# Forgetting attention of six heads issued in the written order on every engine and queue

## The chip, the core and the metric

The kernel runs on one NeuronCore of a Trainium2 chip. The metric is device microseconds (us) of one execution, lower is better. The engines of the core are named as in the profile: PE (matrix products and transposes), DVE (vector engine), ACT (scalar engine), POOL, and SP, whose queue issues all the DMAs of this kernel. Each engine takes its own instructions in the order in which they stand in its program; an instruction whose semaphore has not come yet holds up all that stand behind it on the same engine or queue.

## The reference

One layer of a hybrid decoder on 2048 tokens of width 1024: a normalised, modulated input is projected, three groups of heads mix it (a matrix memory, forgetting attention, spatial gating), an output projection follows, then a convolutional feed-forward block. The part that the change touches is the attention, eight heads of width 64:

```python
F = jnp.cumsum(jax.nn.log_sigmoid(f_pre.astype(jnp.float32)), axis=-1)
for blk in range(s_len // Q_BLOCK):                 # 16 blocks of 128 queries
    lo, hi = blk * Q_BLOCK, (blk + 1) * Q_BLOCK
    logits = (jnp.einsum('bhtd,bhsd->bhts', q[:, :, lo:hi], k[:, :, :hi]) * scale
              + F[:, :, lo:hi, None] - F[:, :, None, :hi])
    logits = jnp.where(mask, logits, -jnp.inf)      # causal
    p = jax.nn.softmax(logits, axis=-1)
    outs.append(jnp.einsum('bhts,bhsd->bhtd', p, v[:, :, :hi]))
```

## The kernel before

The program is written with a framework that sets the semaphores, gives the tiles their buffers, and by default also orders the instructions of each engine: its scheduler takes the written program, and where an instruction is not ready by its own reckoning, it puts a later one that is ready ahead of it. Inside a `tc.manual_schedule()` block every engine and queue keeps the written order instead. The kernel already uses this block for most of the input projections; the attention stands outside it.

The attention runs over heads h = 0 to 7 and, inside a head, over four blocks tb of 512 queries: `phase((h, tb), ...)`. Heads 1 to 6 take tb = 0, 1, 2, 3 in this order; head 0 has only tb = 2 and 3 left here, since its first two blocks are made beside the last input projection; head 7 takes 2, 3, 0, 1.

**`scores` (L190 on).** A block has four rows of 128 queries. A row sees `(tb*4+i+1)*128` keys, taken in parts of at most 1024 columns. One unit is one part: PE makes the logits in a PSUM tile `sp` (L206, two buffers; for 512 columns two products, of the high and the low half of q, then the causal mask by L210), and DVE adds the forget bias and takes the row's extreme in one custom instruction (L212). So a block has 4, 4, 8 and 8 units for tb = 0, 1, 2, 3. When the last part of a row is written, its exponentials follow on ACT (`exps`, L223, one for each part) and the division by the row sum on POOL (L225, L226, L228). These stand in the code behind the `yield` of the unit, so that they are written only when the next unit is asked for.

**`finish` (L234 on).** The product with v, for one block of 128 keys at a time, `(tb+1)*4` units. A unit transposes up to four tiles of the probabilities on PE (L259, into `tp`, three buffers), ACT copies the result as the high half `phi` (L262), DVE subtracts it for the low half `plo` (L263), and PE multiplies both halves with `vv` (L245, L246). The product is held back by three units (the list `behind`): unit j writes the transposes of j and then the product of j-3. There is one PSUM buffer `op` for a block's product; after its last product ACT copies it out as `yo` (L250), and two DMAs store it (L252).

**`phase` (L269 on)** interleaves the scores of one block with the finish of the block before it:

```python
nxt = order[order.index(now) + 1]
kv[nxt] = load_q(*nxt, "qB")                  # four DMAs of q for the next block
n_fin = sum(4 * (t[1] + 1) for t in then)     # units of the block that is finished
for n in range(n_sc):                         # n_sc = 4, 4, 8 or 8 units of scores
    next(sc)
    while done < (n + 1 - lead) * (n_fin - 5) // (n_sc - lead):
        next(fin)
        done += 1
for _ in sc: pass                             # the exponentials of the last row
for _ in fin: pass                            # the rest of the finish
```

So in the written order phase (h, 0) has 2, 3, 3, 3 units of finish behind its four units of scores, phase (h, 1) none (n_fin - 5 is negative), phase (h, 2) 0, 0, 1, 0, 0, 1, 0, 1, phase (h, 3) 0 and then one behind each, and each phase ends with the four or five units of finish that are left.

After the first phase of a head, `load_k(h + 1)` and `load_v(h + 1, range(4))` write the loads of the next head: two DMAs of `kk` (L157), one of `nf` (L158), four of `vv` (L163, 256 KB each). The tag `kvB` has six buffers, three for a head, so head h+1 takes the buffers of head h-1 from h = 2 on. The `q` tiles (tag `qB`, L173, 128 KB for a DMA) have four buffers, two for a block.

Behind the attention stand the output projection (whose weights are loaded by `load_w(0)` in the sixth head), the up projection with its convolution, and the down projection; all of them keep the scheduler's order.

Of the kernel before, what the change touches and what calls it, by code (L numbers as in the profile page):

```python
# [21 lines left out]
NH = 8  # L22
# [11 lines left out]
def trunk(  # L34
# [116 lines left out]
    def load_k(h):  # L151
        tag, e = "kvA" if h == 0 else "kvB", slice(h % 2 * 64, h % 2 * 64 + 64)
        kk = pool.tile([P, S], F32R, name="kk", tag=tag)
        nf = pool.tile([P, S], F32, name="nf", tag=tag)
        vv = pool.tile([P, S // P, P], F32R, name="vv", tag=tag)
        for i in range(2):
            dma(kk[64 * i : 64 * i + 64].bitcast(F32), k_d[h // 2, i, e])  # L157
        dma(nf, nf_d[h : h + 1, :].broadcast_to([P, S]))  # L158
        kv[h] = kk, nf, vv

    def load_v(h, cs):
        for c in cs:
            dma(  # L163
                kv[h][2][:, 4 * c : 4 * c + 4].bitcast(F32),
                v_d[c * TB : (c + 1) * TB, h, :].rearrange("(n p) d -> p n d", p=P),
            )

    def load_q(h, tb, tag):
        q2 = []
        for n in range(2):  # L170
            t = pool.tile([P, TB], F32R, name="q", tag=tag)
            for i in range(2):
                dma(  # L173
                    t[64 * i : 64 * i + 64].bitcast(F32),
                    q_d[h // 2, n, h % 2 * 64 : h % 2 * 64 + 64, tb * TB : (tb + 1) * TB],
                )
            q2.append(t)
        return q2
# [55 lines left out]
    def finish(h, tb, rows):  # L234

        ns = (tb + 1) * 4
        vv = kv[h][2]

        got = []

        def product(j, c0, hi, lo):
            if j == 0:
                got.append(pp.tile([P, 512], F32, name="op", tag="op"))
            op = got[0]
            T.matmul(op[:, c0:], vv[:, j, :], hi[:, c0:], start=(j == 0), stop=False)  # L245
            T.matmul(op[:, c0:], vv[:, j, :], lo[:, c0:], start=False, stop=(j == ns - 1))  # L246
            if j == ns - 1:
                yo = pool.tile([P, 512], F32, name="yo", tag="yo")

                A.copy(yo, op)  # L250
                for n, d in enumerate((yt_d, y2_d)):
                    dma(d[h * 64 : h * 64 + 64, tb * TB : (tb + 1) * TB], yo[64 * n : 64 * n + 64])  # L252

        for j in range(ns):
            i0 = max(0, j - tb * 4)
            c0 = i0 * P
            tp = pp.tile([P, 512], F32, name="tp", tag="tp")
            for i in range(i0, 4):
                T.transpose(tp[:, i * P : (i + 1) * P], rows[i][j // 8][:, (j % 8) * P : (j % 8 + 1) * P], ident)  # L259
            hi = pool.tile([P, 512], F32R, name="phi", tag="phl")  # L260
            lo = pool.tile([P, 512], F32R, name="plo", tag="phl")
            A.copy(hi[:, c0:], tp[:, c0:])  # L262
            V.tensor_tensor(lo[:, c0:], tp[:, c0:], hi[:, c0:].bitcast(F32), op=ALU.subtract)  # L263
            behind.append(lambda j=j, c0=c0, hi=hi, lo=lo: product(j, c0, hi, lo))
            if len(behind) > 3:
                behind.pop(0)()
            yield

    def phase(now, then, lead=0):  # L269

        rows = []
        sc, n_sc = iter(()), 0
        if now:
            sc, n_sc = scores(*now, kv.pop(now) if now in kv else load_q(*now, "qB"), rows), (4, 4, 8, 8)[now[1]]
            if now in order and now != order[-1]:
                nxt = order[order.index(now) + 1]
                kv[nxt] = load_q(*nxt, "qB")
        n_fin = sum(4 * (t[1] + 1) for t in then)
        fin = (u for t in then for u in finish(*t))
        done = 0  # L280
        for n in range(n_sc):
# [4 lines that stand above are left out]
        for _ in sc:  # L286
            pass
        for _ in fin:
            pass
        return now and [(*now, rows)]  # L290

    def wout_open_right():
        pool.open("wo_r", "right", ("yhl0", 2048, 16), ("ld", 2048, 3), ("wo0", 2048, 16))

    def load_split(src, tag, eng, more=None):
        t = pool.tile([P, TB], F32, name="ld", tag="ld")
        dma(t, src)
        if more is not None:
            t2 = pool.tile([P, TB], F32, name="ld", tag="ld")
            dma(t2, more)  # L300
            eng.tensor_tensor(t, t, t2, op=ALU.add)
        hi = pool.tile([P, TB], F32R, name=tag + "h", tag=tag)
        lo = pool.tile([P, TB], F32R, name=tag + "l", tag=tag)
        split(hi, lo, t, eng)
        return hi, lo
# [3 lines left out]
    def load_w(nb):  # L309
        for k in range(KT):  # L310
            src = w_out[k * P : (k + 1) * P, nb * 512 : nb * 512 + 512]
            wo.append(load_split(src, "wo%d" % nb, (G, V)[k % 2]))
# [757 lines left out]
    written = ExitStack()  # L1070
# [57 lines left out]
    for h in range(NH):  # L1128
        for n, tb in enumerate(TBS if h == NH - 1 else (2, 3) if h == 0 else range(4)):
            if (h, n) == (NH - 2, 1):  # L1130
                pool.close("att_r")
                wout_open_right()
            if (h, n) == (NH - 2, 3):
                load_w(0)
            last = phase((h, tb), last, 3 if (h, n) == (0, 0) else 0)
            if n == 0 and h < NH - 1:
                load_k(h + 1)
                load_v(h + 1, range(4))
# [607 lines left out]
```

## Time and profile before

| what | value |
|---|---|
| median of the runs | 2610.47 us (three runs, 2605.68 to 2610.91) |
| profiled execution | 2607.8 us, span of its instructions 2606.1 us |
| mean granted clock of PE | 0.997 |
| the scores' products on PE, first to last | 672.8 to 1111.3 us |
| period of a head, heads 1 to 4 | 51.66 to 51.68 us |

The attention takes the stretch from about 700 to 1125 us of the span, a sixth of the time; the phases that the change touches, (0, 3) to (5, 3), have their scores on PE between 724.7 and 996.7 us. The profile's line numbers (L206 and so on) are those of the kernel before; in the changed kernel all lines behind L1134 stand four lower.

### The profile page before, as it was taken

What the parts mean: (1) busy time and instruction counts of PE and PEld (TensorE: products, weight loads), DVE (VectorE), ACT (ScalarE), POOL (GpSimd) and SP (SyncE); (2) the same over time, 40 slices, a digit from 0 to 9 for tenths busy, and PEclk for the clock granted to TensorE, in tenths of its full rate; (3) what the DMA queues carried; (4) which work ended last, traced back from release to release, by engine and by line L of the source; (5) the groups of instructions that cost most, each with busy time, mean ns of one, the idle gap of its engine ahead of it and who ended that gap; (6) DMA issues with size and microseconds to landing.
All of it is one profiled execution on the core that took longest, in us unless ns stands there. A gap on an engine that the chain in (4) does not pass through costs nothing.

```text
span 2606.1 us, 36311 instructions
## 1 busy us (share of the span) xinstructions
PE 2530.5 (97%) x12521; PEld 2097.9 (81%) x12537; DVE 2010.0 (77%) x3438; ACT 1272.8 (49%) x2424; POOL 402.5 (15%) x532
## 2 busy tenths in 40 slices
PE   5999999999999999999989999999999999999999
PEld 5888888888787877777868888888888888888787
DVE  7657666476388889866589888888888887997797
ACT  4333343432388878844455544454444444444443
POOL 2012310132266556520000000000000000000000
PEclk9999999999999999999999999999999999999999
DMA  7345763454664445266632222255222217658523
GB/s 247 107 120 160 209 209 88 129 152 138 180 164 123 129 126 166 58 195 224 248 89 92 79 89 82 81 201 187 90 81 81 90 65 279 210 176 290 184 93 117
DMA packets 302592, 379.58 MB, mean 146 GB/s; under 512 B 31934, under 2 KB 194588, under 8 KB 300360
## 3 DMA queue, kind: packets, MB, share of 16 engines
q1 hardware_dynamic: 302408, 377.26, 46.1%
q8 instruction: 99, 1.62, 0.3%
q14 instruction: 85, 0.70, 0.1%
HBM read 276.44 MB, written 100.74 MB: 145 GB/s over the span
## 4 chain that ended last, share of the span: by engine, by line
PE 81%; DVE 9%; DMA 4%; ACT 3%; issue 2%; POOL 1%; SPq 0%; DVEq 0%; ACTq 0%; POOLq 0%
PE ub L56 11%; PE ub L54 11%; PE ub L55 11%; PE acc L54 6%; PE acc L56 6%; PE acc L55 6%; PE db L55 4%; PE db L56 4%; PE db L54 4%; PE sp L206 3%; PE tp L259 3%; PE op L245 2%; PE op L246 2%; PE wps L55 2%; PE wps L54 2%
## 5 line engine op out<-in xcount | busy, mean ns | idle before, releaser
L54 PE MATMUL acc<-wh,hh 128*128 128x512 f32 (+2 forms) x768 | 285.5, 373 | 1.9 <-DVE vhl L762 1.2
L54 PE MATMUL ub<-T,wsph 128*128 128x512 f32 x704 | 274.2, 390 | 5.8 <-ACT wsph L1358 5.8
L56 PE MATMUL ub<-T,wspl 128*128 128x512 f32 x704 | 273.7, 389 | 1.6 <-DVE wspl L1359 1.6
L56 PE MATMUL acc<-wh,hl 128*128 128x512 f32 (+2 forms) x768 | 274.2, 360 | 0.3 <-DVE hl L566 0.3
L55 PE MATMUL acc<-wl,hh 128*128 128x512 f32 (+2 forms) x768 | 273.9, 358 | 0.2
L55 PE MATMUL ub<-T,wsph 128*128 128x512 f32 x704 | 273.9, 389 | 0.0
L55 PE MATMUL db<-wspl,wsph 128*128 128x512 f32 x616 | 240.6, 391 | 3.6 <-DVE wspl L1490 3.5
L56 PE MATMUL db<-wsph,wspl 128*128 128x512 f32 x616 | 239.6, 389 | 0.0
L54 PE MATMUL db<-wsph 128*128 128x512 f32 x616 | 238.3, 389 | 0.3 <-ACT wsph L1489 0.3
L1358 ACT CAST wsph<-S 128x512 fp32r<-128x512 f32 x176 | 109.7, 623 | 228.4 <-PE ub L55 162.8
L263 DVE TENSOR_TENSOR plo<-tp,phi 128x512 fp32r<-128x512 f32 (+1 forms) x320 | 187.0, 607 | 31.6 <-ACT phi L262 29.4
L54 PE MATMUL ub<-B,wsph 128*128 128x512 f32 x528 | 207.1, 392 | 2.8 <-ACT wsph L1358 2.8
L56 PE MATMUL ub<-B,wspl 128*128 128x512 f32 x528 | 207.2, 392 | 0.6 <-DVE wspl L1359 0.6
L55 PE MATMUL ub<-B,wsph 128*128 128x512 f32 x528 | 207.0, 392 | 0.0
L223 ACT ACTIVATE L<-L,nm 128x1024 f32<-128x1024 f32 (+2 forms) x192 | 172.6, 903 | 36.0 <-DVE nm L212 34.7
L262 ACT CAST phi<-tp 128x512 fp32r<-128x512 f32 (+1 forms) x320 | 160.0, 521 | 40.2 <-PE tp L259 38.9
L259 PE MATMUL tp<-ident,L 128*128 128x128 f32 x1088 | 177.0, 274 | 2.5 <-POOL L L228 0.6
L206 PE MATMUL sp<-kk,q 128*128 128x512 f32 (+3 forms) x640 | 169.2, 375 | 3.3 <-DVE nm L212 2.2
L1489 ACT CAST wsph<-act 128x512 fp32r<-128x512 f32 x132 | 82.3, 623 | 179.0 <-PE db L55 162.2
L228 POOL TENSOR_SCALAR L<-L,rs 128x1024 f32<-128x1024 f32 (+2 forms) x192 | 167.2, 881 | 11.0
L56 PEld LDWEIGHTS acc<-wh,hl 128*128 128x128 f32 x768 | 145.0, 190 | 22.3 <-DVE hl L566 0.8
L54 PEld LDWEIGHTS acc<-wh,hh 128*128 128x128 f32 x768 | 146.2, 191 | 20.7 <-DVE vhl L762 1.4
(333 smaller groups left out, 5942.9 us busy)
## 6 DMA issues: line engine op xcount, KB each, us to landing
w<-in_w_up_dram SPq DMA_DIRECT2D x88, 512.0 KB
wd<-in_w_down_dram SPq DMA_DIRECT2D x176, 256.0 KB
wa<-in_w_ada_dram SPq DMA_DIRECT2D x96, 256.0 KB
act_d<-yc SPq DMA_DIRECT2D x44, 512.0 KB
act<-act_d SPq DMA_DIRECT2D x44, 512.0 KB
wr<-in_w_in_dram SPq DMA_DIRECT2D x64, 256.0 KB
q<-q_d SPq DMA_DIRECT2D x128, 128.0 KB
hc_d<-hl SPq DMA_DIRECT2D x28, 512.0 KB
```

Of the source, the lines that this page charges most:

```text
L54: T.matmul(ps, lh, rh, start=start, stop=False, skip_group_check=resume)
L55: T.matmul(ps, lh, rl, start=False, stop=False, skip_group_check=resume)
L56: T.matmul(ps, ll, rh, start=False, stop=stop, skip_group_check=resume)
L206: T.matmul(sp[:, b : b + bw], q2[n][:, qs], kk[:, s0 + b : s0 + b + bw], start=n == 0, stop=n == 1 and not last)
L223: A.activation(L[c], L[c], AF.Exp, bias=nm[:, n - 1 : n], scale=-1.0, accum_out=rs[:, c : c + 1])
L228: G.tensor_scalar(t, t, rs[:, 0:1], 1.0, op0=ALU.mult, op1=ALU.mult)
L245: T.matmul(op[:, c0:], vv[:, j, :], hi[:, c0:], start=(j == 0), stop=False)
L259: T.transpose(tp[:, i * P : (i + 1) * P], rows[i][j // 8][:, (j % 8) * P : (j % 8 + 1) * P], ident)
L262: A.copy(hi[:, c0:], tp[:, c0:])
L263: V.tensor_tensor(lo[:, c0:], tp[:, c0:], hi[:, c0:].bitcast(F32), op=ALU.subtract)
L1358: A.copy(hi, src)
L1489: A.copy(hi, v)
```

## The change

Four lines in the loop over the phases. The block of written order is entered ahead of phase (0, 3), the second of head 0, and left ahead of phase (6, 0). In between, PE, DVE, ACT, POOL and SP's DMA queue keep the order in which the code writes them. No instruction is added, removed or changed in size.

```diff
             if (h, n) == (NH - 2, 3):
                 load_w(0)
+            if (h, n) == (0, 1):
+                written.enter_context(tc.manual_schedule())
+            if (h, n) == (NH - 2, 0):
+                written.close()
             last = phase((h, tb), last, 3 if (h, n) == (0, 0) else 0)
             if n == 0 and h < NH - 1:
                 load_k(h + 1)
                 load_v(h + 1, range(4))
```

## The prediction

> **What bounds the kernel now.** I read the page first, then the stretches of single heads, the groups by form in the attention, the waits, and last the order in time of PE, DVE, ACT and SP.
>
> ```profile
> span 2606.1 us, 36311 instructions
> PE 2530.5 (97%) x12521; PEld 2097.9 (81%) x12537; DVE 2010.0 (77%) x3438; ACT 1272.8 (49%) x2424; POOL 402.5 (15%) x532
> PE 81%; DVE 9%; DMA 4%; ACT 3%; issue 2%; POOL 1%; SPq 0%; DVEq 0%; ACTq 0%; POOLq 0%
> ...
> core 0: us, PE busy (x) PEld busy (x) DVE busy (x) ACT busy (x) POOL busy (x), PEclk, DMA share, GB/s
> 863.21:914.89 51.68, 50.64 (x313) 41.33 (x313) 43.88 (x89) 42.06 (x93) 30.81 (x48) 1.00 0.46 123
> ...
> ACT L L223 <- DVE nm L212: 6.2, 6, 1.8
> ACT phi L262 <- PE tp L259: 4.9, 11, 1.7
> ```
>
> The first row gives PE 97% of the span and the chain 81% on PE. The attention is different from the rest: in one head's period (51.68 us, from the stretches) PE is idle 1.0 us, but DVE is busy 43.9 and ACT 42.1. Three engines are nearly full at once, so the order decides. In the two waits, of the same period, ACT waits for the reduction (L212) and for transposes (L259), short each time: something else is put into the holes.
>
> **PE's work in a head.** From starts, since ends of products are modelled:
>
> ```profile
> 906.65 0.48 PE L245 MATMUL op<-phi,vv 128*128 128x512 f32 x1
> 906.98 0.40 PE L246 MATMUL op<-plo,vv 128*128 128x512 f32 x1
> 907.22 0.60 PE L259 MATMUL tp<-ident,L 128*128 128x128 f32 x4
> 907.57 0.48 PE L245 MATMUL op<-phi,vv 128*128 128x512 f32 x1
> ...
> 913.43 1.06 PE L206 MATMUL sp<-kk,q 128*128 128x512 f32 x4
> 914.33 0.23 PE L210 MATMUL sp<-maskb,identb 128*128 128x128 bf16 x1
> 914.40 0.28 PE L259 MATMUL tp<-ident,L 128*128 128x128 f32 x1
> ```
>
> A pair of products takes 0.57 (906.65 to 907.22), four transposes 0.35, scores over 1024 keys 0.90, a mask 0.07. By the loop's counts a head has 136 transposes (11.9), 34 full pairs' worth of products (19.4), 17 times 1024 columns of scores (15.3) and 16 masks (1.1): 47.7 us; by phase tb = 0 to 3 it is 14.7, 5.5, 11.0 and 16.5. The period of 51.68 holds 4.0 us more.
>
> **What the written order adds.** No instruction goes or comes; the change takes away the filling of holes. I walked one head by hand, each instruction starting when its engine is free in the written order, its inputs are there and its buffer is released, with these durations:
>
> ```profile
> L263 DVE TENSOR_TENSOR plo<-tp,phi 128x512 fp32r<-128x512 f32 x218 | 146.0, 688 | 28.0 <-ACT phi L262 26.4
> L262 ACT CAST phi<-tp 128x512 fp32r<-128x512 f32 x218 | 123.8, 585 | 33.2 <-PE tp L259 32.1
> L223 ACT ACTIVATE L<-L,nm 128x1024 f32<-128x1024 f32 x78 | 90.1, 1157 | 16.9 <-DVE nm L212 16.6
> L212 DVE CUSTOM_DVE_ANT_0 L<-sp,nf 128x1024 f32<-128x1024 f32 x70 | 85.3, 1219 | 7.8 <-PE sp L206 5.7 <-PE sp L210 1.4
> ...
> L250 ACT COPY yo<-op 128x512 f32<-128x512 f32 x29 | 17.1, 591 | 0.4 <-PE op L246 0.4
> L223 ACT ACTIVATE L<-L,nm 128x768 f32<-128x768 f32 x14 | 13.2, 942 | 9.0 <-DVE nm L212 9.0
> L212 DVE CUSTOM_DVE_ANT_0 L<-sp,nf,nm 128x768 f32<-128x768 f32 x8 | 8.1, 1016 | 0.9 <-DVE nm L212 0.2
> ```
>
> Behind one another they overlap by some 0.08, so I count 0.61 for plo, 0.5 for phi and yo, 1.15 for a reduction or an exponential over 1024 and 0.95 over 768, and 0.05 to 0.1 for each hand-over.
>
> Phase (h, 1), time from its start. Four units of scores stand with no finish between them, and `sp` has two buffers, so the third and fourth wait for the first and second reduction; PE has all four at 3.6, the fourth reduction ends at 4.8, its exponential at 6.05. Only then comes phi of the first finish unit in ACT's order (6.6), plo at 7.3. PE meanwhile has written three transposes and the three products held back, and stands at 5.5: `tp` has three buffers, and the fourth waits for that plo. Then the new block's first product waits for yo, which stands behind three phi on ACT: 7.9. PE leaves at 8.5 for 5.5 of work: **3.0 lost**.
>
> Phase (h, 2) has three finish units among its eight units of scores. DVE has 4 x 1.15 + 1.9 (the parts of 128 to 512) + 3 x 0.61 + gaps of phi, PE 7.4: PE waits for `sp`. At the end the last row's exponentials (1.7) stand on ACT ahead of five phi, so the fourth transposes of the rest wait again. The walk ends at 15.2 for 11.0: **4.2 lost**.
>
> Phase (h, 3) has a loop for each row: the reduction of its second part (0.97 on average), its two exponentials (1.15 + 0.98), the phi behind them (0.5), its plo (0.61), and behind that plo on DVE the next second part. With hand-overs that is 4.45 a row; PE needs 3.6 a row. Four rows and the five phi behind the last exponentials: 20.6 for 16.5: **4.1 lost**. Phase (h, 0) has short exponentials (0.4 to 0.7) and 16 finish units, PE sets it: 15.0 for 14.7, **0.3 lost**.
>
> Together a head takes 59.3. POOL's division is inside the walk: the rest of the finish covers it at each border.
>
> **The queue of SP.** The built programs differ here in what an engine's own row cannot show. Before, and then after:
>
> ```
> L157 kk x2; L158 nf; L252 yo x2; L173 q x7; L163 vv x4
> L157 kk x2; L158 nf; L163 vv x4; L173 q x4; L252 yo x2
> ```
>
> For h >= 2 the `vv` loads wait for PE: their buffer is read by the last product of (h-1, 3), which in the written order is the third product in phase (h, 1), at 5.5. Behind them on SP stand the four `q` of phase (h, 2), which is 3.0 away. Before, these q went ahead:
>
> ```profile
> 917.10 0.28 PE L246 MATMUL op<-plo,vv 128*128 128x128 f32 x1
> ...
> 903.04 14.35 SPq L173 DMA_DIRECT2D q<-q_d  x7
> 917.49 2.19 SPq L163 DMA_DIRECT2D vv<-v_d  x4
> 921.04 0.60 SPq L173 DMA_DIRECT2D q<-q_d  x1
> 927.27 2.46 SPq L173 DMA_DIRECT2D q<-q_d  x4
> ...
> 922.50:924.50 2.00, 2.00 (x16) 1.65 (x14) 1.54 (x6) 2.00 (x7) 1.24 (x3) 1.00 0.89 285
> 924.50:925.50 1.00, 0.95 (x9) 0.71 (x8) 0.84 (x2) 1.00 (x6) 1.00 (x3) 1.00 0.06 20
> 930.30:931.30 1.00, 1.00 (x7) 0.83 (x6) 0.82 (x2) 1.00 (x5) 0.70 (x3) 1.00 0.59 182
> 931.30:932.30 1.00, 1.00 (x8) 0.86 (x7) 1.00 (x4) 0.69 (x3) 0.82 (x3) 1.00 0.05 18
> ```
>
> The last product starts at 917.10, vv follows at 917.49. Four vv take 2.2 to issue; four q take 4.1 from first issue (927.27) to the end of traffic (931.3). So q is there 0.4 + 2.3 + 4.1 = 6.8 after that product, at 12.3 instead of 8.5: **3.8** for each of heads 2 to 5. Head 1 is free of it: its vv take fresh buffers, and no wait for PE stands on them. Bounds: nothing, if other work holds PE until 12.3; 5.5, if q also queues behind vv's traffic, which ended 7.0 after vv's first issue. I keep 3.8, the plain sum. The yo stores also stand ahead of later q's, but those have a phase of 15 us or more to land.
>
> **The clock after such a hole.** PE's granted clock (the column of 1.00 above) does fall in this kernel behind the attention:
>
> ```profile
> 1227.30:1230.70 3.40, 1.25 (x12) 1.01 (x10) 1.63 (x4) 0.98 (x2) 0.00 (x0) 1.00 0.45 130
> 1230.70:1234.10 3.40, 3.03 (x12) 2.66 (x13) 3.29 (x6) 3.40 (x6) 0.00 (x0) 0.50 0.76 213
> ```
>
> After 3.4 us in which PE was busy 1.25, the next 3.4 ran at half clock. A hole of 3.8 in (h, 1) will do the same; the first two scores of 0.90 that open phase (h, 2) then take twice as long before DVE's waits cover the rest: **1.8**, bounds 0 and 3.4 x 0.5 x 2 windows = 3.4. The Trainium skill's page "TensorE: Matmul & The Clock Gate", Part 1, asks for a whole idle window of about 3.4 us of a free-running clock, which a hole of 3.8 seldom covers; by it the 1.8 would mostly be missing, 4 x 1.8 = 7 us less in the sum. The row above shows a fall after a window that was a third busy, so I go by the row.
>
> **The sum.** Heads 2 to 5: 59.3 + 3.8 + 1.8 - 51.7 = 13.2 each, 52.8. Head 1: 59.3 - 51.7 = 7.6. Phase (0, 3), the first inside, costs like a (h, 3) phase, less what the period before already loses there: 3. Heads 6 and 7 and all behind them keep their order: 0, with 3 either way for the filling work of the output weights that moves. Together 63. The profiled execution took 2607.8 (span 2606.1 and 1.7 around it), so 2671; the median of the runs is 2.7 above that execution, inside their spread of 5.2, and I say 2672.
>
> **Rivals.**
> *The clock holds* (0.15): as forecast, but PE is never idle for a whole window, and its clock stays at 1.00: 63 - 4 x 1.8 = 56, 2664. For it: the other holes of the walk are under 2 us, and the record before in the attention is 1.00 throughout. Against: the half clock behind a window that was busy 1.25 of 3.4. It is the rule of the page named above.
> *The loads are covered* (0.16): the walk holds, but q lands before PE asks, so neither the 3.8 nor the 1.8 comes: 5 x 7.6 + 3 = 41, 2649. For it: heads where ACT and DVE run later than I walked leave PE busy until 12.3. Against: nothing else stands ahead of phase (h, 2) on PE.
> *Only the loads cost* (0.13): the holes of ACT and DVE are filled in the written order too, because the three units of delay are enough, and only 3.8 + 1.8, and 1.0 a head for small waits, are left: 4 x 5.6 + 5 = 27, 2635. For it: the waits above are short. Against: 4.45 against 3.6 a row is a loop, which delay cannot hide.
> *Faster* (0.04): the loop of a phase (h, 3) row is in truth below 3.6, where PE decides again, and whole pairs of products and sets of transposes, unbroken as in 906 to 908, carry PE at its own pace. Then up to 4.0 a head goes, 5.3 heads: 21, 2587. By the busy row alone only 1.0 a head could go, 2602. The Trainium skill ("Trainium Kernel Development and Optimization", Performance Expectations) calls matmul busy time "a bad metric" because matmuls are pipelined; by that the larger gain is the open one. Against it stand DVE 43.9 and ACT 42.1 in chains.
> *It does nothing* (0.02): the two orders agree in effect. The rows of the built programs differ on all five, so hardly.
>
> **How the numbers follow.** The forecast has 0.50 and spans 2651 to 2700 (the walk's losses a third less or a quarter more, q up to 5.5, clock up to 3.4). The range goes down to 2632 to take in both rivals on the same side and ends at 2702. About 0.2%, 5 us, can be told from no change. Slower 0.94, the same 0.02, faster 0.04.
>
> **What would show it.** Right: a head's period near 65 from head 2 on and near 59 for head 1; PE waiting at L206 for the DMA of q once a head, four times, some 4 us each, and half clock behind it; SP's vv waiting for L246 with q behind; PE at L259 waiting for plo about 2 us in each (h, 1); DVE at L212 and ACT no longer above 75% busy. Wrong: a period under 55, no wait of PE for q, or ACT busy as before in the same share.

## The result: 2705 us, slower by 3.8%

The changed kernel takes 2705.0 us (median of 4 runs, 2702.4 to 2710.0), the kernel before 2608.2 (4 runs, 2605.7 to 2610.9): ratio 1.0378, 95% interval 1.0362 to 1.0393. Forecast were 2672 and 2632 to 2702: the sign came, and so did each mechanism that was forecast, but the loss is 97 us instead of 64, and the time lies 3 us above the range.

The page of the changed kernel. Its profiled execution took 2710.0 us, the longest of the four; that of the kernel before took 2607.8, so that the two profiles are 102 us apart and not 97:

```profile
span 2708.3 us, 36287 instructions
PE 2568.0 (95%) x12537; PEld 2117.2 (78%) x12537; DVE 2016.1 (74%) x3438; ACT 1280.1 (47%) x2424; POOL 401.8 (15%) x532
PE 53%; DVE 8%; DMA 4%; issue 3%; ACT 3%; POOL 1%; SPq 1%; DVEq 0%; ACTq 0%; POOLq 0%
...
L263 DVE TENSOR_TENSOR plo<-tp,phi 128x512 fp32r<-128x512 f32 (+1 forms) x320 | 188.5, 608 | 86.6 <-ACT phi L262 85.0
L259 PE MATMUL tp<-ident,L 128*128 128x128 f32 x1088 | 181.9, 283 | 32.8 <-DVE plo L263 31.2
L206 PE MATMUL sp<-kk,q 128*128 128x512 f32 (+3 forms) x640 | 179.2, 403 | 31.4 <-DMA q<-q_d 19.5
```

DVE and ACT do the same work as before (2016 against 2010 us, 1280 against 1273). PE's busy time rose by 37 with the same work, which goes with a lower clock, and its share of the chain fell from 81% to 53%. New are the last two waits: PE at the transposes (L259) for `plo`, 31.2 us, and at the scores (L206) for the DMA of `q`, 19.5 us.

Stretches from the first score of phase (1, 0) to that of phase (6, 0), in the kernel before (first row) and the changed one, and then, of the changed one, the heads from one phase (h, 1) to the next (columns as in the prediction):

```profile
738.39:996.69 258.30, 253.15 (x1561) 206.54 (x1560) 219.69 (x441) 211.16 (x463) 154.69 (x242) 1.00 0.46 125
```

```profile
750.66:1098.03 347.37, 284.36 (x1543) 222.67 (x1542) 220.12 (x434) 214.26 (x455) 151.85 (x236) 0.89 0.35 94
...
767.00:833.68 66.68, 57.40 (x312) 45.15 (x311) 44.61 (x88) 43.37 (x92) 30.91 (x48) 0.90 0.36 93
833.68:905.98 72.30, 57.97 (x314) 45.25 (x312) 44.64 (x88) 43.38 (x93) 30.93 (x48) 0.88 0.32 88
905.98:978.00 72.02, 58.49 (x315) 45.56 (x314) 44.97 (x89) 43.39 (x92) 30.96 (x48) 0.88 0.32 88
```

PE's wait for q from 725 to 1095 us (in total, times, longest):

```profile
PE sp L206 <- DMA q<-q_d: 19.5, 4, 5.2
```

The five heads went from 258.3 to 347.4: 89 of the 102 us. Head 1 takes 66.7 (forecast 59), the next two 72 (forecast 65). The wait for q comes four times, as forecast, of up to 5.2 us. Ahead of them, (1, 0) begins 12.3 later, of which 2.4 were there already when head 0 began; the 9.9 between stand at phase (0, 3), the first in the written order, but not all of them are its cost (see below).

### The profile page after: what moved, and what is told of

It reads as the page before. It is cut to its first block, busy times and chain, and to the rows that moved or that the text cites. A ratio compares the mean times of both kernels' runs of the same rounds, so it can differ in the third digit from the quotient of the medians.

```text
span 2708.3 us, 36287 instructions
## 1 busy us (share of the span) xinstructions
PE 2568.0 (95%) x12537; PEld 2117.2 (78%) x12537; DVE 2016.1 (74%) x3438; ACT 1280.1 (47%) x2424; POOL 401.8 (15%) x532
## 4 chain that ended last, share of the span: by engine, by line
PE 53%; DVE 8%; DMA 4%; issue 3%; ACT 3%; POOL 1%; SPq 1%; DVEq 0%; ACTq 0%; POOLq 0%
PE ub L56 10%; PE ub L55 10%; PE ub L54 10%; PE db L55 4%; PE db L56 4%; PE db L54 4%; PE sp L206 3%; PE tp L259 3%; DVE L L212 2%; DVE wspl L1494 2%; PE op L245 1%; PE op L246 1%; ACT L L223 1%; PE wps L56 1%; PE wps L54 1%
## 5 line engine op out<-in xcount | busy, mean ns | idle before, releaser
L259 PE MATMUL tp<-ident,L 128*128 128x128 f32 x1088 | 181.9, 283 | 32.8 <-DVE plo L263 31.2
L206 PE MATMUL sp<-kk,q 128*128 128x512 f32 (+3 forms) x640 | 179.2, 403 | 31.4 <-DMA q<-q_d 19.5
L259 PEld LDWEIGHTS tp<-ident,L 128*128 128x128 f32 x1088 | 132.8, 145 | 69.3 <-DVE plo L263 43.3
L206 PEld LDWEIGHTS sp<-kk,q 128*128 128x128 f32 x640 | 124.2, 208 | 66.5 <-DMA q<-q_d 22.8
L212 DVE CUSTOM_DVE_ANT_0 L<-sp,nf 128x1024 f32<-128x1024 f32 (+7 forms) x128 | 125.8, 986 | 64.4 <-PE sp L206 49.0
```

What stands on the lines that cost most here:

```text
L206: T.matmul(sp[:, b : b + bw], q2[n][:, qs], kk[:, s0 + b : s0 + b + bw], start=n == 0, stop=n == 1 and not last)
L212: V.tensor_tensor_reduce(out=L[c], in0=sp[:, :w], in1=nf[:, s0 : s0 + w], scale=-1.0, scalar=3.0e38 if c == 0 else nm[:, 0:1], op0=ALU.add ...
```

## Experiments

Theory 1 in the expectations is the prediction's account (chains of ACT and DVE, q behind vv, the clock), with sizes read from the changed kernel's trace. The edits are shown shortened, against the changed kernel. Differences in us are between medians, on a base of 2608; each median is good to some 4 us by its interval.

**Without SP.**

```diff
-tc.manual_schedule()
+tc.manual_schedule(engines={PE, DVE, Activation, Pool})
```

> Written order on PE, DVE, ACT and POOL in the same phases, while SP's DMA queue stays with the scheduler, which puts the four q loads of phase (h, 2) ahead of the vv loads again. Theory 1 (a head of the changed kernel loses some 20.6 us: about 8 to chains of ACT and DVE, 5.2 to q behind vv, 7.3 to the half clock that follows the holes): the wait for q goes (4 x 5.2 = 21) and with it about half of the half clock of heads 2 to 5 (4 x 3 = 12), so 2705 - 33 = 2672. Theory 2 (the clock costs nothing, since DVE and ACT set the pace): 2705 - 21 = 2684. Theory 3 (another wait takes the place of that for q): 2700.

2677.4 us, ratio 1.0268 [1.0251, 1.0285]. SP's part is worth 28 us. What stays is 70, where the walk had 41. Head 2 of this run has no wait for q and the full clock throughout, so its phases (1, 2, 3 and the next head's 0) can be laid beside the walk:

```profile
834.45:843.32 8.87, 6.58 (x39) 5.15 (x38) 6.12 (x13) 6.21 (x14) 5.63 (x8) 1.00 0.26 77
843.32:859.23 15.91, 12.57 (x71) 9.52 (x70) 11.02 (x24) 10.92 (x25) 9.53 (x17) 1.00 0.44 123
859.23:881.22 21.99, 18.20 (x103) 13.55 (x102) 15.61 (x29) 14.77 (x30) 10.76 (x17) 1.00 0.38 89
881.22:896.80 15.58, 14.99 (x103) 12.61 (x102) 11.93 (x25) 11.22 (x26) 4.98 (x9) 1.00 0.35 114
```

Walked were 8.5, 15.2, 20.6 and 15.0. Each is short, by 0.4, 0.7, 1.4 and 0.6, together 62.35 against 59.3. The same run shows the loop of a (h, 3) row, on ACT in order of time:

```profile
862.73 1.15 ACT L223 ACTIVATE L<-L,nm 128x1024 f32<-128x1024 f32 x1 [0.63 <-DVE nm L212]
...
863.88 0.81 ACT L223 ACTIVATE L<-L,nm 128x640 f32<-128x640 f32 x1
...
864.69 1.05 ACT L262 CAST phi<-tp 128x512 fp32r<-128x512 f32 x2
...
867.00 1.15 ACT L223 ACTIVATE L<-L,nm 128x1024 f32<-128x1024 f32 x1 [0.78 <-DVE nm L212]
...
876.28 1.15 ACT L223 ACTIVATE L<-L,nm 128x1024 f32<-128x1024 f32 x1 [1.54 <-DVE nm L212]
```

and on DVE:

```profile
865.28 0.69 DVE L263 TENSOR_TENSOR plo<-tp,phi 128x512 fp32r<-128x512 f32 x1 [0.91 <-ACT phi L262]
865.89 1.01 DVE L212 CUSTOM_DVE_ANT_0 L<-sp,nf,nm 128x768 f32<-128x768 f32 x1
```

Exponential at 862.73, the second at 863.88, phi behind it at 864.69, plo at 865.28 after DVE had waited 0.91, behind plo the next row's reduction at 865.89, and the next exponential at 867.00, for which ACT waited 0.78. From the first row's exponential to the fourth's it is 4.52 a row; walked was 4.45. So the loop was right, and in (h, 3) the walk is short at the ends of the phase: the first exponential comes 3.5 in, and behind the fourth's start PE needs 4.9 until it leaves, 8.4 for which the walk left 7.2.

**SP alone.**

```diff
-tc.manual_schedule()
+tc.manual_schedule(engines={SP})
```

> Written order on SP's DMA queue alone, the four compute engines stay with the scheduler. Theory 1: the scheduler knows of the late q and puts other work there, some of it wrongly timed: 2610 to 2630. Rival: the hole cannot be filled, since the scores of phase (h, 2) need q whatever is put ahead: 4 x (5.2 + 5 of half clock) = 41, 2650.

2635.1 us, ratio 1.0109 [1.0094, 1.0124]: 28.5, which is 5 above the lower of the two forecasts (2610 to 2630). With the 70 of the run above that is 98, so the two halves add up to the whole within the noise. But what PE waits for changes (725 to 1095 us):

```profile
PE tp L259 <- POOL L L228: 10.8, 21, 1.8
PE op L245 <- ACT yo L250: 5.5, 10, 1.0
PE sp L206 <- DVE nm L212: 5.3, 9, 1.5
PE tp L259 <- DVE plo L263: 4.6, 7, 0.8
PE sp L206 <- DMA q<-q_d: 0.5, 2, 0.4
```

PE waits for q hardly at all: in its order of time the scheduler has put finish units there. The largest wait is now that of the transposes (L259) for POOL's division. That the rows made from the late q are what comes late there is a reading of these waits, not tested by a run of its own.

**All engines, `vv` later.**

```diff
-load_v(h + 1, range(4))                     # after phase (h, 0)
+load_v(h + 1, range(4))                     # heads 2 to 5: after phase (h, 1), behind q
```

> The changed kernel with load_v(h + 1) written one phase later for heads 2 to 5, so that the q of phase (h, 2) stands ahead of vv on SP; all else in the written order as before. Theory 1: no wait of PE for q, half clock in phase (h, 2) down to the 6.8 us that head 1 shows: 2705 - 33 = 2672, and a period near head 1's 66.7 for heads 2 to 5 in place of 72.2. Theory 2 (clock free): 2684. Theory 3 (another wait in its place): 2700.

2677.1, ratio 1.0269 [1.0254, 1.0284], 28 less than the changed kernel, just what SP's freedom gave: SP's whole cost is the `vv` issue with q behind it. Head 2 takes 64.8; no wait for q is left in it, and of PE's waits the one for plo is the largest (6.2 us; the reduction has 1.7, yo 1.6):

```profile
833.48:898.27 64.79, 55.00 (x313) 42.94 (x312) 44.78 (x88) 43.11 (x93) 30.91 (x48) 0.95 0.37 97
```

**PE alone, and ACT with DVE alone.**

```diff
-tc.manual_schedule()
+tc.manual_schedule(engines={PE})              # one run
+tc.manual_schedule(engines={Activation, DVE}) # the other
```

> Written order on PE alone in the same phases; DVE, ACT, POOL and SP stay with the scheduler. Theory C (the 71 us that are left without SP's part come from the written order of ACT and DVE, where a copy phi stands behind exponentials and a reduction behind plo): with those two free most of it goes, 2620 to 2635. Rival D (PE's own order costs: it no longer fills its holes with later work): most of it stays, 2660 to 2677.

> Written order on ACT and DVE alone; PE, POOL and SP stay with the scheduler. Theory C: most of the 71 us comes, 2660 to 2677. Rival D: PE fills the holes, 2620 to 2635.

2642.8 (ratio 1.0135 [1.012, 1.015], +35) and 2653.3 (1.0177 [1.0156, 1.0198], +45). Both fell between the two theories: neither PE's order nor that of ACT and DVE makes the 70 alone; together they give 80. A head with PE alone in written order:

```profile
862.34:920.40 58.06, 51.37 (x314) 41.20 (x313) 44.44 (x89) 42.70 (x93) 31.09 (x49) 1.00 0.40 108
```

DVE's wait for phi in about a head, of this run and then of the one with ACT and DVE alone:

```profile
DVE plo L263 <- ACT phi L262: 8.6, 12, 2.0
```

```profile
DVE plo L263 <- ACT phi L262: 13.6, 16, 2.4
```

58.1 is 6.4 over before at full clock, of the 10.7 that a head loses there without SP. By its phases, from the first scores on PE, (h, 1) takes 8.4, (h, 2) 15.5, (h, 0) 15.6, nearly as with all engines, but (h, 3) 18.6 instead of 22. So in three phases PE's order is enough for nearly the whole loss, and in (h, 3) the order of ACT and DVE has to come to it for the whole loop; with that order DVE waits for phi in a head as long as in the changed kernel (13.8). In (h, 1) the walk had put phi behind the last exponential; with PE alone in written order ACT makes phi first, and the phase is only 0.5 shorter.

**A finish unit in (h, 1).** With `vv` later, one finish unit is written behind the second of the four units of scores and one behind the fourth, ahead of the last exponentials, to break the row of four scores of which the walk made 3.0 lost.

```diff
-while done < (n + 1 - lead) * (n_fin - 5) // (n_sc - lead):
+while done < (n + 1 - lead) * (2 if n_fin == 4 else n_fin - 5) // (n_sc - lead):
```

> The changed kernel with the vv loads one phase later (2677) and, in phase (h, 1), two of the four finish units written between the four units of scores and not all behind them. If the hole of phase (h, 1) comes from its order alone (transposes wait 2.1 us for plo behind the fourth row's exponentials, then 0.9 for yo), it shrinks by about 2.5 a head: 2665. Rival: the units that leave the end of phase (h, 1) uncover the last row's exponentials and division ahead of the next finish, and the time stays at 2677 or rises.

2686.2, ratio 1.0298 [1.0282, 1.0313]: no gain. The median is 9 above that without the edit, but in the two profiles the phases in written order, (0, 3) to the start of (6, 0), take the same (343.8 and 344.7 us). At full clock phase (h, 1) takes 9.06, against 8.9 without the edit, because the wait moved to `op`, which is not free until yo is copied behind the exponentials (PE's waits in about a head):

```profile
PE op L245 <- ACT yo L250: 4.5, 3, 3.0
PE tp L259 <- DVE plo L263: 4.1, 4, 2.0
```

**Shorter exponentials, first try.** With `vv` later; the exponentials of heads 0 to 5 over 128 columns only, the row sum to the power zero. The kernel leaves out the other columns' exponentials, so these heads do not compute the attention.

```diff
-A.activation(L[c], L[c], AF.Exp, ...)
+A.activation(L[c][:, :128], L[c][:, :128], AF.Exp, ...)
-G.tensor_scalar(t, t, rs[:, 0:1], 1.0, op0=ALU.mult, op1=ALU.mult)
+G.tensor_scalar(t, t, rs[:, 0:1], 1.0, op0=ALU.mult, op1=ALU.min)
```

> The changed kernel with the vv loads one phase later (2677), where for heads 0 to 5 each exponential on ACT is made over 128 columns only, instead of 128 to 1024, and the division's result is capped at 1 with a row sum taken as 1 (numbers stay finite; the output of these heads is not the reference's). Same number of instructions and same order on all engines. Theory C: an exponential takes some 0.4 us in place of up to 1.15, the loop of a row (reduction, exponentials, phi, plo, next reduction) falls below what PE needs, and a head goes from 64.5 to about 54: 2677 - 5 x 10 = 2627. Rival D (PE's order and DVE's reductions set the pace): 2665.

2808.8, ratio 1.0765, and no answer: the `min` put in to keep numbers finite made POOL the bound (busy 75.0 of the 84.8 us of a head).

**Shorter exponentials, second try.** The same with a second factor of 1e-30 instead of the `min`.

> As the kernel with the vv loads put later (2677), but the exponentials of heads 0 to 5 go over the first 128 columns only (0.40 us instead of 0.4 to 1.15), the division by the row sum is taken with exponent zero, and its second factor is 1e-30; the other columns of the probabilities stay logits. Theory R (the loop of a row, through the exponentials on ACT, sets the pace in phases (h, 1) to (h, 3)): a (h, 3) row falls from over 4.5 to 3.2, below PE's 3.6, so (h, 3) goes from 22 or 23 to about 17, (h, 1) loses 0.8 and (h, 2) 1.2: heads of 57 to 58, 2630 to 2645. Theory O (the order of PE and DVE alone sets the pace, ACT only waits in between): heads above 62, 2665 or more. POOL: if its second operation was what took 2.65 us in the earlier try, it is back at 0.88; if the data did it, it stays.

2633.9, ratio 1.0104 [1.0087, 1.012]: 43 less than with full exponentials. Head 2, and its phase (h, 3):

```profile
813.55:868.85 55.30, 50.98 (x313) 41.19 (x312) 44.31 (x88) 32.13 (x92) 31.25 (x48) 1.00 0.42 115
...
836.08:853.26 17.18, 17.04 (x103) 13.88 (x102) 15.34 (x29) 9.76 (x30) 11.27 (x18) 1.00 0.23 67
```

POOL's division over 1024 columns in about a head, of this run and of the first try:

```profile
L231 POOL TENSOR_SCALAR L<-L,rs 128x1024 f32<-128x1024 f32 x12 | 13.5, 1122 | 1.2
```

```profile
L231 POOL TENSOR_SCALAR L<-L,rs 128x1024 f32<-128x1024 f32 x8 | 29.6, 3705 | 0.7
```

In (h, 3) PE is busy 17.04 of 17.18: the loop is gone, as forecast (about 17). Heads take 55.3 (forecast 57 to 58) and the clock is 1.00 throughout the attention. So 43 of the 70 us that the compute engines lose, the half clock behind the chains' holes among them, hang on the length of the exponentials, not on ACT's total, which fills 43 of 65 us and is not full. The run shortens all exponentials, those in the loops and those at the ends of phases; it does not tell the two apart.

**Warm PE over the hole.** The changed kernel with products of no use at the end of (h, 1), heads 2 to 5: 22 of them, then 15.

```diff
+if n == 1 and 2 <= h <= 5:
+    for _ in range(22):                       # 15 in the second run
+        T.matmul(junk, kk[:, 0:P], kk[:, 0:512], start=True, stop=True)
```

> The changed kernel with 22 products more on PE (kk by kk, 512 columns, into a tp buffer that nobody reads, about 22 x 0.23 = 5 us) at the end of phase (h, 1) of heads 2 to 5, where PE stands and waits for q. They do no useful work: they keep PE busy in the hole. Theory 1: the wait for q stays, but the 13.7 us of half clock behind it shrink to 3.4 or none, so some 5 us a head: 2705 - 20 = 2685. Theory 2 (the half clock is hidden behind DVE and ACT): 2705, or some us more.

> The changed kernel with 15 products of no use at the end of phase (h, 1) of heads 2 to 5 instead of 22. They begin 8.9 us into the phase and take 3.5 to 5, so they end before q comes at 14.2, and phase (h, 2) starts no later than in the changed kernel. If the half clock is worth the 3.0 to 4.7 a head by which the phases behind the hole are longer than at full clock, 2705 falls by 12 to 18, to 2687 to 2693. If other work covers the half clock, as much as with 22 products or less is gained: 2697 or more.

2697.6 (ratio 1.0353 [1.0336, 1.0371]) and 2697.0 (1.0339 [1.0323, 1.0354]), 7 to 8 less than the changed kernel each, 2 us a head, against a noise of some 4 in each median. In the profiles the phases in written order take 363.4 and 364.7 us, against 374.1 of the changed kernel. The 22 began at 836.38, ran 6.78 us and made (2, 1) 1.2 longer than in the changed kernel (1.6 on average of the four heads); the 15 end before q comes and delay nothing (PE in order of time, then the stretch of head 2):

```profile
840.73 3.57 PE L1146 MATMUL junk<-kk 128*128 128x512 f32 x15
844.95 0.47 PE L206 MATMUL sp<-kk,q 128*128 128x512 f32 x1 [0.65 <-DMA q<-q_d]
```

```profile
831.86:900.64 68.78, 57.87 (x328) 45.03 (x327) 44.68 (x88) 43.11 (x92) 30.90 (x48) 0.98 0.34 92
```

By the number that is the second case of the expectation, other work that covers the half clock. The phases tell more. Behind the hole, (h, 2) takes 18.8 to 19.0 us in the changed kernel and 15.9 to 16.2 with the 22 products, at full clock in all four heads: some 3 us a head are the price of the half clock there, and the products that run too long give about half of it back. With the 15, one stretch of half clock stays in (3, 2) and one in (5, 2). So the 2 a head are what warming gains here, and less than what the half clock costs.

## Why the prediction was right in sign and 33 us short

Two steps of the sum failed: the walk's chains, put at 7.6 us a head and measured at 10.7, and the clock, charged behind the hole of q alone with 7 us and measured at 23, half of it behind other holes.

**The walk's chains: right mechanism, mis-sized.** 59.3 was walked, 62.35 is measured at full clock without the q wait, so 10.7 a head is lost instead of 7.6: 53 for five heads where the sum had 38. Each phase was walked 4 to 7% short, (h, 3) most, and there not in the loop of a row (4.52 against 4.45) but before its first and behind its last exponentials. The wait of PE at L259 for `plo` in (h, 1), forecast as about 2 us, is there:

```profile
841.54 0.33 PE L259 MATMUL tp<-ident,L 128*128 128x128 f32 x1 [2.09 <-DVE plo L263]
```

**Phase (0, 3): about as put.** The sum had 3, with half a sentence and no row. By the first scores it is 9.9 (12.3 less 2.4), but the edges of the written order move work. Phases (0, 3) and (5, 3) of the run without SP:

```profile
724.72:751.47 26.75, 22.24 (x122) 17.27 (x123) 19.67 (x38) 19.99 (x43) 16.29 (x25) 0.95 0.97 260
1053.57:1069.49 15.92, 14.48 (x85) 11.55 (x84) 13.38 (x24) 12.04 (x24) 9.43 (x12) 1.00 0.44 132
```

The first holds 122 instructions of PE, the last 85, and (2, 3) between them 103: at the entry work is still to be done that the scheduler had put off, and at the exit the scores of (6, 0) go ahead of the finish again. So (5, 3) is 6.1 shorter than (2, 3) at the same clock, and of the 9.9 some 3 to 4 are left.

**q behind vv: right, at the wrong end.** SP of the changed kernel, then PE, at the hole of head 2:

```profile
839.48 2.01 SPq L163 DMA_DIRECT2D vv<-v_d  x4
841.54 2.86 SPq L173 DMA_DIRECT2D q<-q_d  x4
```

```profile
839.17 0.28 PE L246 MATMUL op<-plo,vv 128*128 128x128 f32 x1
...
847.91 2.54 PE L206 MATMUL sp<-kk,q 128*128 128x512 f32 x6 [5.22 <-DMA q<-q_d]
```

The last product is at 5.5 of the phase (833.68), as walked, and vv follows 0.3 later, as before. But q is there 8.7 after that product instead of 6.8: that fits the case that the prediction had set as its upper bound (5.5), q queued behind vv's traffic as well as behind its issue. Over the four heads the wait is 19.5 where the sum had 15.2.

**The clock: right behind the hole, missing elsewhere.** The stretches of 3.41 us in which the granted clock changes, changed kernel, head 2:

```profile
840.50:843.91 3.41, 1.06 (x3) 0.43 (x3) 1.76 (x4) 1.67 (x5) 2.25 (x3) 1.00 0.80 226
843.91:847.32 3.41, 0.00 (x0) 0.00 (x0) 0.00 (x0) 0.00 (x0) 0.00 (x0) 0.50 1.06 270
847.32:850.74 3.42, 2.67 (x7) 1.92 (x7) 0.58 (x1) 0.00 (x0) 0.00 (x0) 0.50 0.59 196
850.74:854.15 3.41, 2.70 (x9) 2.21 (x9) 1.60 (x5) 1.63 (x4) 0.34 (x2) 0.50 0.00 0
854.15:857.56 3.41, 3.41 (x13) 2.89 (x11) 1.89 (x6) 1.85 (x4) 1.87 (x3) 0.50 0.00 0
857.56:860.97 3.41, 3.31 (x23) 2.52 (x22) 3.24 (x6) 2.47 (x6) 2.33 (x4) 1.00 0.00 0
884.90:888.31 3.41, 1.36 (x9) 0.79 (x7) 1.60 (x3) 3.02 (x8) 1.84 (x4) 0.99 0.00 0
888.31:891.72 3.41, 3.41 (x16) 3.12 (x15) 1.42 (x6) 0.85 (x2) 1.11 (x2) 0.51 0.00 0
```

The clock falls behind a stretch that was busy 1.06, not only behind the idle one, and again at 888.31 behind 1.36, at the end of (h, 3), where there are only the holes of the chains. The prediction had left these out as under 2 us; by its own row (busy 1.25 of 3.40, so idle 2.15) holes of about 2 us in one stretch are enough. So the rival that the clock holds is out, and the row of the prediction (1.25 busy, then half clock) decided rightly against the whole idle window of the Trainium skill's page "TensorE: Matmul & The Clock Gate", Part 1. The price behind the q hole was put at 1.8 a head and is 3 (the run with 22 products): 12 for four heads where the sum had 7. What was missing are the other holes. The phases in written order, from the first score of (0, 3) to that of (6, 0), before, without SP, and in the changed kernel (before, (0, 3) begins at 721.48; the 724.7 given for it above is a later product of its first row):

```profile
721.48:996.69 275.21, 270.06 (x1665) 220.94 (x1666) 235.78 (x472) 226.76 (x497) 166.57 (x261) 1.00 0.49 132
```

```profile
724.72:1069.49 344.77, 293.97 (x1664) 231.10 (x1665) 240.83 (x472) 233.16 (x497) 168.80 (x260) 0.95 0.39 107
```

```profile
723.92:1098.03 374.11, 306.58 (x1664) 239.93 (x1665) 239.79 (x472) 234.28 (x498) 168.10 (x261) 0.89 0.36 98
```

At full clock they would take about 331, an estimate: four heads of 62.35, the phases (5, 0) to (5, 3) at 15.6, 8.9, 15.9 and 15.9, and (0, 3) at 25.6 (its 26.75 less the 1.1 by which a phase (h, 3) with a like share of half clock is longer, 23.1 against 22.0). So without any wait for q some 13 us go to the clock. In the changed kernel 374.1 less 331 less the 19.5 of q leaves 23: the 12 behind the hole of q, and 11 elsewhere.

**The account.** Forecast and measured, over these phases of the changed kernel: chains 38 and 53, phase (0, 3) 3 and 3, wait for q 15 and 19.5, clock behind it 7 and 12, clock elsewhere 0 and 11. The sums are 63 and 99, of which the chains and the clock have 31 of the 36 that were missing. The 53 come from one head of the run without SP, and the last term is what was left over, so that the sum of the measured terms had to agree.

**The rivals.** "Only the loads cost" was priced at 2635, and the run with SP alone, where the other engines may fill their holes, took 2635.1: in a kernel that is not the changed one, so that its price came out is luck, and its condition (that delay in the written order fills the holes) was wrong. "The loads are covered" would have been 2649; the run that takes the loads out of the way is at 2677, and the 28 between are the same mis-sized chains (15) and the clock at the other holes (13). "Faster" failed at its condition: a (h, 3) row takes 4.52, not under 3.6.

**Open** is how PE's order and that of ACT and DVE share the loss within phases (h, 1) and (h, 2): alone they cost 35 and 45, with POOL 70 together. POOL's order alone was not run.

## What to carry to other kernels

When three engines are nearly full, a written order that is fixed for all of them makes loops across engines (here exponential, copy, subtraction, next reduction); walk one turn of the loop, but add the ends of the phase too, where in (h, 3) most of the walk's error lay. On a queue that serves several kinds of loads, a load that waits for a buffer delays what stands behind it at issue and, as the 8.7 us instead of 6.8 suggest, by the traffic it brings as well; one line that puts it behind the urgent load took back 28 of 97 us. Freeing one engine at a time in otherwise equal kernels splits such a loss cheaply. Where one row shows the clock fall behind a partly busy stretch, charge it at every hole of that size, not at the longest alone. And when phases are compared across the edge of an order, count the instructions in them: work that only moved looks like cost.

## What the hardware showed unexpectedly

The clock is slow to come back: in the rows above, two stretches busy 2.67 and 2.70 of 3.4 at half clock were each followed by another at half clock, and only one that was busy throughout (854.15) ended it. In the run with `vv` later stretches busy 2.81 (842.09) and 3.04 (814.78) ended it too. The cost is less than the time at half clock suggests: with 15 products the half clock in the attention went from 81.9 us to 37.5, and the time by 8 (9.4 in the phases in written order). The Trainium skill's page "TensorE: Matmul & The Clock Gate", Terms, puts the penalty at about the throttled time times 1 − K/N, with 4/8 for the half clock; as an estimate that would be 22 us here. Part of the difference is in the rows: in the stretch at 843.91 PE had nothing to do, so that its half clock cost nothing. How the rest divides is not shown.

POOL's `tensor_scalar` over 1024 columns took 3.71 us with multiply and minimum, and 1.12 with multiply and multiply on operands of the same shape and type (the second factor was 1.0 and 1e-30).
